# One queue for all transfers of a two-layer decoder step: SyncE issues every DMA, loads are queued when their buffer is free

## The chip, the core and the metric

The kernel runs on one core of a Trainium2 chip. That core has a matrix engine (TensorE, PE in the profile), a vector engine (VectorE, DVE), a scalar engine (ScalarE, ACT), a general one (GpSimd, POOL) and a fifth that only issues transfers and waits (SyncE, SP). Each executes its own list of instructions in order and waits on semaphores for the others. The metric is the device time of one execution in microseconds (us); lower is better.

## The reference

The program is one inference step of a two-layer decoder, for 512 prompt columns and 64 sample columns (8 sequences of 8 tokens) that share all weights. D_MODEL is 1024, and everything is float32. Cut to what matters here:

```
for l in range(2):                              # DEPTH
    h = rmsnorm(x)
    z = h @ w_in[l]                             # all inputs of the mixers, and 4 gates per channel
    A = dilated sliding-window attention, 3 groups of 4 heads; the sample also reads cached keys / values
    B = sliding-window grouped-query attention, 8 heads, window 128; the sample reads its cache
    C = Bc * conv_w3(Cc * hc)                   # the sample starts from state_c_conv
    D = GLU(GELU(Re(C x) + D u)),  x = scan of a complex diagonal state (S5)
    x = x + rmsnorm((sum of gate_i * (branch_i @ W_i)) @ w_out[l])
    x = x + rmsnorm(swiglu(rmsnorm(x)))
    x = x + (p[l] @ w_ple) * sigmoid(x @ w_ple_gate)
return x, and the caches and states moved on by the new positions
```

## The kernel before

**Weights.** All weight products are made with the 576 columns as two halves of 288 (`HS`). A product is three passes of TensorE, high weight times high input, high times low and low times high, so that float32 precision is kept with the fp32r type. Weights arrive as 636 blocks of 128 x 512 (`wblk`, 256 KB each). `load_blk` queues one into a ring of four raw buffers (`wr`, `NRAW`). `split_blk` takes a raw block apart: ACT copies it, rounded, into `wh`, and POOL (or DVE) subtracts to give `wl`; these rings have eight buffers each (`NSPL`). `gemms` emits the products, 24 of 288 columns for a block, 15264 in all, and `pump` queues loads and splits of later blocks whenever a block has had its last product.

**Order.** The program is straight-line code. While it is built, `track` keeps a planned clock for each engine (E, V, S, P, and Q for SyncE) and one for the memory, with a cost for each instruction, and the builder asks these clocks what to emit next: whether VectorE or GpSimd takes an operation (`pick`), and whether a side task may go on (`wait`, `soon`, `calm`). The side tasks are Python generators: the state-space work (`ssm_u`, `ssm_pair`, `ssm_sample`), attention of the prompt (`a_task`, `b_task`), attention of the sample (`sa_task` for mixer A, `sb_task` for B). `tick` advances them between two products of a GEMM, `drain` advances them with no product between when something must be finished first. `PACE` holds numbers that tune this, one set for each layer. What the builder decided is then fixed: each engine executes its list in that order.

**Transfers.** Two engines issue them. `sync` is SyncE: it carries the weight blocks, the stores of new keys and values, states and results, and the copies of the old caches to their outputs (`old_a_k<-cache_a_k` and the like, from DRAM to DRAM). `side_dma` issues all other loads and the scratch traffic from ACT's list: cached keys and values (`kcA`, `vcA`, 52 blocks of 256 KB each in a layer; `kcB`, `vcB`, the mask `mSB`), the three stacked copies of the state-space input that go out to DRAM scratch and come back (`uscr`), their parameters (`bT`, `cT`, `x0`), and the previous convolution inputs (`cpv<-convprev`). `sa_task` keeps up to `PRE` of its blocks queued ahead (6 in the first layer, 7 in the second). A transfer's completion semaphore is one of eight, handed out in the order of the program over both queues, so a transfer waits until the one eight before it has landed.

**Around the change.** The first layer begins with `Gc+A0` and has its state-space work in the background of `A0` and `A1+B`; the second begins with `Gc`. `ep_conv` (mixer C) fetches the convolution state into `cpv`, has POOL copy it to `zcs`, later has POOL gather the new state in `cst` and stores it (`convo`). In the profile all instructions carry line 256, that of the helper that records them, so the names of the tiles tell them apart: `s` are general slots, `bk` PSUM banks, `rc`, `zsw` and `ast` small temporaries.

Of the kernel before, what the change touches and what calls it, by code (L numbers as in the profile page):

```python
# [19 lines left out]
L = 2  # L20
T = 576
# [140 lines left out]
NPAR = 73  # L162
# [105 lines left out]
def _free(ap):  # L268
    n = 1
    for st, c in list(ap.ap)[1:]:  # L270
# [6 lines left out]
    dict(CALM=5.12, ACALM=1.91, RES=6, LOBIAS=11.89, SLACK=-0.07, SIDE_MAX=4, MARGIN=0, PRE=6,  # L277
         CONC=(1, 3, 1, 2, 2), XCALM=0.3, SQP=0.15, NEAR=-0.03, SCALM=4.55, SN=7, HOLD=True, BATCH=1, GR=2),
    dict(CALM=2.03, ACALM=0, RES=1, LOBIAS=8.29, SLACK=0.52, SIDE_MAX=3, MARGIN=3, PRE=7,
         CONC=(3, 4, 2, 2, 1), XCALM=0.3, SQP=-0.3, NEAR=-0.6, SCALM=0, SN=2, HOLD=False, BATCH=1, GR=1),  # L280
# [3 lines left out]
class Build:  # L284
    NS = 63
    NSPL = 8
    SN = 2
# [23 lines left out]
    NEXT = 5  # L311
# [6 lines left out]
    def __init__(self, nc, tc, A, stack):  # L318
# [15 lines left out]
        self.p0 = 0.0  # L334
        self.lat, self.rby = {}, {}
# [45 lines left out]
    def track(self, eng, op, a, k):  # L381
# [20 lines left out]
        if op == "dma_start":  # L402
            self.clk[eng] = t + 0.06
# [4 lines left out]
            e = d + 0.6  # L408
        else:
# [241 lines left out]
    def pump(self):  # L651
        while self.done_blk < self.total_blk and self.uses[self.done_blk] == 0:
            self.wh.pop(self.done_blk)
            self.wl.pop(self.done_blk)
            self.done_blk += 1
        while self.next_split < min(self.total_blk, self.done_blk + self.NSPL):
            if self.next_load <= self.next_split:
                self.load_blk(self.next_load)
                self.next_load += 1
            self.split_blk(self.next_split)  # L660
            self.next_split += 1
        while self.next_load < min(self.total_blk, self.next_split + self.NRAW):
            self.load_blk(self.next_load)
            self.next_load += 1
# [4 lines left out]
    def gemms(self, l, units, half, xs, there=None):  # L669
# [3 lines left out]
        for i in range(n):  # L673
# [4 lines left out]
            for un, bk in zip(units, bks):  # L678
# [9 lines left out]
                if i < n - 1:  # L688
                    if not self.uses[b]:
                        self.pump()  # L690
                    next(self.pre, None)
# [51 lines left out]
    def side_dma(self, o, i):  # L743
        self.S.dma_start(o, i)
# [32 lines left out]
def build(nc, tc, A, stack):  # L777
# [418 lines left out]
    for l in range(L):  # L1196
# [76 lines left out]
        def ep_qkv(un, half, bk):  # L1273
            n, key = un.name, un.key
            c0, w = HS[half]
            if n in ("qa", "ka"):
# [5 lines left out]
                def go():  # L1282
# [3 lines left out]
                    if half == 1:  # L1286
                        while (n, key, 0) not in done:
                            yield None
                        t = (qs if n == "qa" else ks)[:, 2 * key[0] + key[1], :]
# [6 lines left out]
            elif n in ("qb", "kb"):  # L1296
# [10 lines left out]
                def go():  # L1307
# [3 lines left out]
                    if half == 1:  # L1311
                        while (n, key, 0) not in done:
                            yield None
                        if n == "kb":
                            sync.dma_start(A["kvB"][l, 0], s.t)
# [3 lines left out]
            elif n in ("va", "vb"):  # L1319
# [13 lines left out]
                if half == 1:  # L1333
                    o = A["kvA"][l, 1, key[0], key[1]] if n == "va" else A["kvB"][l, 1]
                    sync.dma_start(o, s.t)
                    done.add(("T", n, key))
# [21 lines left out]
        def ep_conv(un, half, bk):  # L1358
# [4 lines left out]
            elif n == "cc":  # L1363
                t = bk.t
                V.tensor_tensor(t[:, :w], bk.t[:, :w], rs1.t[:, c0:c0 + w], OP.mult)
                if i not in zcp:
# [3 lines left out]
                    pv = B.tmp("cpv", 2, (128, 8, 2))  # L1370
                    B.side_dma(pv, A["convprev"][l, :, i])
# [7 lines left out]
                else:  # L1379
# [7 lines left out]
                    cst_ = B.tmp("cst", 2, (128, 18))  # L1387
                    P_.tensor_copy(cst_[:, 0:2], z[:, 512:514])
                    P_.tensor_copy(cst_[:, 2:18].rearrange("p (b k) -> p b k", b=8), zs[:, :, 8:10])
                    sync.dma_start(A["convo"][l, :, i], cst_)  # L1390
# [8 lines left out]
                    B.drop(zcp[i][0])  # L1399
# [39 lines left out]
        def ssm_pair(js):  # L1439
# [6 lines left out]
            for n, j in enumerate(js):  # L1446
                for k in range(3):
                    B.side_dma(braw[n][32 * k:32 * k + 32], A["bT"][l, j])
# [116 lines left out]
        def ssm_sample(jj):  # L1565
# [38 lines left out]
            sync.dma_start(A["ssmS"][l, jj], xs_)  # L1604
# [9 lines left out]
            V.tensor_tensor(xp[:, 1], w1, w2, OP.add)  # L1614
            sync.dma_start(A["ssmP"][l, jj], xp)
            yield from B.wait(X.t, cr.t)
# [853 lines left out]
def make_inputs(inp):  # L2470
# [20 lines left out]
    par[:, :, 72] = np.tile(np.repeat(f["attn_sinks"].reshape(L, 8), 8, axis=1), (1, 2))  # L2491
    m["par"] = par
# [10 lines left out]
    m["bT"], m["cT"] = bT, cT  # L2503
    x0 = np.stack([f["state_d_re"], f["state_d_im"]], 1)
    m["x0"] = np.ascontiguousarray(x0.reshape(L, 2, 8, 2, 4, 128).transpose(0, 3, 5, 1, 4, 2))
    m["convprev"] = np.ascontiguousarray(f["state_c_conv"].reshape(L, 8, 2, 2, 128).transpose(0, 4, 3, 1, 2))
# [71 lines left out]
```

## Time and profile before

| | |
|---|---|
| three runs | 2486.67, 2488.82 and 2489.55 us, median 2488.82 |
| the profiled execution | 2490.76 us; its span, first to last instruction, is 2489.0 |
| PE, DVE, ACT, POOL busy | 2364.5, 1188.9, 985.3, 918.9 us |
| granted TensorE clock, mean over the span | 0.976 of full speed |

Busy time counts neither waits nor the issuing of transfers, which the profile puts on a separate line of the engine's sequencer (ACTq, SPq). A PE that counts as busy can still run at half its clock.

### The profile page before, as it was taken

To read this page: it belongs to the slowest core of one execution; us is meant where nothing else is said; L and a number is where in the kernel's file an instruction comes from. 1 tells how busy PE (TensorE), PEld (TensorE's weight loads), DVE (VectorE), ACT (ScalarE), POOL (GpSimd) and SP (SyncE) were. 2 spreads that over 40 slices of the span, in tenths; PEclk is the share of its full clock that TensorE was granted. 3 is DMA by queue.
4 is the path that set the end of the run, shared out by engine and by line. 5 is a ranking of instruction groups with operands and counts; after the bars stand their busy time and mean duration, and the time that the engine had idled before them with its cause. 6 is when DMAs were issued, how large, how long until landed. Compare 5 with 4: busy or idle time off the path is not lost.

```text
span 2489.0 us, 48194 instructions
## 1 busy us (share of the span) xinstructions
PE 2364.5 (95%) x18686; PEld 2248.7 (90%) x18686; DVE 1188.9 (48%) x3126; ACT 985.3 (40%) x2230; POOL 918.9 (37%) x936
## 2 busy tenths in 40 slices
PE   8899799999999999999997989999999999999999
PEld 8788688877999999999897988998779999999999
DVE  7986897532426220223637798665224342102343
ACT  4333546422346332334532255754223543223342
POOL 5435242222333444433323364422223334344332
PEclk9999899999999999999998999999999999999999
DMA  5334343775453434434444454535874634343332
GB/s 181 100 109 136 105 141 116 247 248 178 136 170 114 119 111 131 125 115 130 142 146 140 127 163 136 154 128 163 278 266 148 203 89 119 115 138 117 115 93 73
DMA packets 164246, 358.94 MB, mean 144 GB/s; under 512 B 25808, under 2 KB 35024, under 8 KB 158800
## 3 DMA queue, kind: packets, MB, share of 16 engines
q1 hardware_dynamic: 118576, 279.08, 36.6%
q10 hardware_dynamic: 45440, 76.77, 9.3%
q8 instruction: 147, 2.41, 0.4%
q14 instruction: 83, 0.68, 0.1%
HBM read 331.59 MB, written 113.43 MB: 179 GB/s over the span
## 4 chain that ended last, share of the span: by engine, by line
PE 73%; DVE 13%; DMA 5%; ACT 3%; issue 3%; POOL 1%; ACTq 1%; SPq 0%; DVEq 0%; POOLq 0%
PE bk L256 73%; DVE s L256 8%; DVE bk L256 4%; DMA s<-vcA 2%; ACT s L256 2%; DMA wr<-wblk 1%; ACTq L256 1%; POOL wl L256 1%; POOL s L256 1%; DMA old_a_k<-cache_a_k 1%; DMA s<-kcA 0%; ACT wh L256 0%; DVE sin L256 0%; DMA cpv<-convprev 0%; DMA s<-uscr 0%
## 5 line engine op out<-in xcount | busy, mean ns | idle before, releaser
L256 PE MATMUL bk<-s,wh 128*128 128x288 f32 x10176 | 2084.0, 300 | 55.0 <-ACT s L256 19.1
L256 PEld LDWEIGHTS bk<-s,wh 128*128 128x128 f32 x10176 | 1647.7, 190 | 95.6 <-issue 29.0
L256 PE MATMUL bk<-s,wl 128*128 128x288 f32 x5088 | 1511.4, 297 | 8.2 <-POOL wl L256 8.2
L256 POOL TENSOR_TENSOR wl<-wr,wh 128x512 fp32r<-128x512 f32 x634 | 817.5, 1297 | 1422.9 <-ACT wh L256 1341.6
L256 PEld LDWEIGHTS bk<-s,wl 128*128 128x128 f32 x5088 | 967.1, 190 | 9.0 <-POOL wl L256 9.0
L256 DVE TENSOR_TENSOR bk<-bk,s 128x288 f32<-128x288 f32 (+2 forms) x620 | 287.5, 481 | 670.3 <-PE bk L256 648.9
L256 ACT ACTIVATE wh<-wr 128x512 fp32r<-128x512 f32 x636 | 396.2, 631 | 392.1 <-PE bk L256 216.2
L256 ACT ACTIVATE s<-bk 128x288 f32<-128x288 f32 (+5 forms) x434 | 171.3, 414 | 414.9 <-DVE bk L256 242.3
L256 PE MATMUL bk<-s,s 128*32 128x128 f32 (+10 forms) x2736 | 192.2, 319 | 32.9 <-DVE s L256 16.8
L256 ACT ACTIVATE zsw<-bk 32x288 f32<-32x288 f32 (+1 forms) x360 | 144.7, 403 | 138.6 <-DVE bk L256 89.7
L256 PEld LDWEIGHTS bk<-s,s 128*32 128x32 f32 (+5 forms) x2736 | 111.3, 130 | 89.5 <-issue 44.1
L256 ACT ACTIVATE rc<-bk 128x288 f32<-128x288 f32 x128 | 52.3, 409 | 278.9 <-DVE bk L256 207.0
L256 DVE TENSOR_TENSOR s<-s,bk 128x288 f32<-128x288 f32 (+1 forms) x226 | 95.1, 440 | 92.3 <-ACT bk L256 89.4
L256 DVE SCALAR_TENSOR_TENSOR s<-bk,s 128x288 fp32r<-128x288 f32 (+1 forms) x184 | 83.0, 456 | 63.1 <-ACT s L256 62.3
L256 PE MATMUL bk<-ident,s 128*128 128x128 f32 (+1 forms) x406 | 65.6, 296 | 20.0 <-ACT s L256 11.5
L256 DVE SCALAR_TENSOR_TENSOR bk<-rc,bk 128x288 f32<-128x288 f32 x96 | 44.2, 460 | 74.1 <-PE bk L256 38.9
L256 PEld LDWEIGHTS bk<-ident,s 128*128 128x128 f32 (+1 forms) x406 | 48.7, 146 | 32.6 <-ACT s L256 14.1
L256 DVE TENSOR_TENSOR s<-bk,s 128x512 f32<-128x512 f32 (+3 forms) x124 | 66.1, 572 | 24.9 <-PE bk L256 24.6
L256 DVE TENSOR_TENSOR s<-s,s 128x32 f32<-128x32 f32 (+8 forms) x221 | 73.7, 375 | 6.5 <-DMA s<-cT 4.4
L256 DVE COPY s<-bk 128x512 f32<-128x512 f32 (+5 forms) x102 | 47.2, 471 | 61.8 <-PE bk L256 40.5
L256 ACT ACTIVATE s<-bk,par 128x288 fp32r<-128x288 f32 (+1 forms) x80 | 41.4, 517 | 63.5 <-PE bk L256 35.0
L256 ACT ACTIVATE s<-s,bst 128x256 f32<-128x256 f32 (+1 forms) x87 | 40.1, 473 | 43.6 <-DVE bst L256 43.6
(114 smaller groups left out, 976.0 us busy)
## 6 DMA issues: line engine op xcount, KB each, us to landing
wr<-wblk SPq DMA_DIRECT2D x636, 256.0 KB
old_a_k<-cache_a_k SPq DMA_DIRECT2D x128, 255.0 KB
old_a_v<-cache_a_v SPq DMA_DIRECT2D x128, 255.0 KB
s<-kcA ACTq DMA_DIRECT2D x104, 256.0 KB
s<-vcA ACTq DMA_DIRECT2D x104, 256.0 KB
old_a_k<-cache_a_k SPq DMA_DIRECT2D x32, 252.0 KB
old_a_v<-cache_a_v SPq DMA_DIRECT2D x32, 252.0 KB
kvA<-s SPq DMA_DIRECT2D x24, 288.0 KB
```

Source lines behind the costliest of these rows:

```text
L256: r = f(*a, **k)
```

## The change

1. `side_dma` issues from SyncE. ACT issues no transfer any more (376 before).
2. A new `fetch`, called from `pump` and between the products of a GEMM, queues a weight block only when the planner thinks that the last reader of its raw buffer is nearly done; before, `pump` queued it as soon as the ring's numbering allowed.
3. The planner gives a transfer 0.4 us of issue instead of 0.06, and holds the ninth open transfer of SyncE's queue until the first has landed (`lanes`). `NEXT` and the numbers in `PACE` are other ones; `sa_task` queues 8 blocks ahead in the second layer (7 before).
4. GpSimd's copies of new queries, keys and convolution state, and the stores of `kvA`, `kvB`, `convo`, `ssmS` and `ssmP`, are emitted when the planner thinks that their data is there (`B.wait`), as side tasks where they weren't.
5. The convolution state comes as 32 more columns of the parameter tile `par`, so the four `convprev` loads are gone.
6. `bT` is stacked three times on the host: one load of 96 x 256 in place of three of 32 x 256 (48 become 16).

The number of weight products and their order are unchanged, and so is the other arithmetic.

```diff
@@ -274,10 +274,10 @@
 PACE = (
...
-    dict(CALM=2.03, ACALM=0, RES=1, LOBIAS=8.29, SLACK=0.52, SIDE_MAX=3, MARGIN=3, PRE=7,
-         CONC=(3, 4, 2, 2, 1), XCALM=0.3, SQP=-0.3, NEAR=-0.6, SCALM=0, SN=2, HOLD=False, BATCH=1, GR=1),
+    dict(CALM=1.41, ACALM=0.0, RES=1, LOBIAS=14, SLACK=0.21, SIDE_MAX=3, MARGIN=3, PRE=8,
+         CONC=(2, 4, 2, 2, 2), XCALM=0.3, SQP=0.23, NEAR=-0.6, SCALM=0, SN=5, HOLD=True, BATCH=1, GR=1),
@@ -400,12 +401,17 @@
             t = max(t, self.fin.get(y, self.base.get(y[0], 0.0)) + (0.0 if f[1] == eng else f[0]),
                     self.rdt.get(y, 0.0) + (0.0 if self.rby.get(y, eng) == eng else 0.13))
         if op == "dma_start":
-            self.clk[eng] = t + 0.06
+            if eng == "Q":
+                self.lanes.append(0.0)
+                t = max(t, self.lanes.popleft())
+            self.clk[eng] = t + 0.4
             by = n * list(outs[0].ap)[0][1] * 4 / 340e3
             lat = 0.1
             self.clk["D"] = max(self.clk["D"], self.now) + by
             d = max(self.clk["D"], t + 1.4 + by)
             e = d + 0.6
+            if eng == "Q":
+                self.lanes[-1] = e
         else:
             lat = 0.13
             if eng == "E":
@@ -659,7 +665,13 @@
                 self.next_load += 1
             self.split_blk(self.next_split)
             self.next_split += 1
+        self.fetch()
+
+    def fetch(self):
         while self.next_load < min(self.total_blk, self.next_split + self.NRAW):
+            old = self.ring.get(("wr", self.ring.get(("n", "wr"), 0) % self.NRAW))
+            if self.last.get(old, 0.0) > self.now + 0.2:
+                break
             self.load_blk(self.next_load)
             self.next_load += 1
 
@@ -688,6 +700,7 @@
                 if i < n - 1:
                     if not self.uses[b]:
                         self.pump()
+                    self.fetch()
                     next(self.pre, None)
                     self.nt += 1
                     self.tick(self.nt % self.BATCH == 0)
@@ -741,7 +754,7 @@
             self.RES if any(st["q"] for st in self.streams[1:]) else 0), "room")
 
     def side_dma(self, o, i):
-        self.S.dma_start(o, i)
+        self.Q.dma_start(o, i)
 
     def booked(self):
         return sum(max(0, a[1]) for st in self.streams for a in st["act"])
@@ -1286,6 +1299,7 @@
                     if half == 1:
                         while (n, key, 0) not in done:
                             yield None
+                        yield from B.wait(s.t)
                         t = (qs if n == "qa" else ks)[:, 2 * key[0] + key[1], :]
                         P_.tensor_copy(t, s.t[:, 512:576])
                         if n == "ka":
@@ -1312,6 +1326,7 @@
                         while (n, key, 0) not in done:
                             yield None
                         if n == "kb":
+                            yield from B.wait(s.t)
                             sync.dma_start(A["kvB"][l, 0], s.t)
                         done.add((n, key))
 
@@ -1332,8 +1347,13 @@
                     ep_scale(bk, s.t[:, c0:c0 + w], half)
                 if half == 1:
                     o = A["kvA"][l, 1, key[0], key[1]] if n == "va" else A["kvB"][l, 1]
-                    sync.dma_start(o, s.t)
-                    done.add(("T", n, key))
+
+                    def go():
+                        yield from B.wait(s.t)
+                        sync.dma_start(o, s.t)
+                        done.add(("T", n, key))
+
+                    B.task(go())
 
         def v_task(n, key):
             s = vT.pop((n, key))
@@ -1367,8 +1387,7 @@
                     B.room(1)
                     zcp[i] = (B.slot(), cp.tile([128, 80], F32, name=B.nm("zcs"), tag=f"zcs{i}"))
                     V.memset(zcp[i][0].t[:, 0:2], 0.0)
-                    pv = B.tmp("cpv", 2, (128, 8, 2))
-                    B.side_dma(pv, A["convprev"][l, :, i])
+                    pv = pr[:, 73 + 16 * i:89 + 16 * i].rearrange("p (b k) -> p b k", b=8)
                     zs = zcp[i][1].rearrange("p (b k) -> p b k", b=8)
                     P_.tensor_copy(zs[:, :, 0:2], pv)
                 z = zcp[i][0].t
@@ -1384,10 +1403,6 @@
                     B.pdrop(bk)
                     B.drop(hcs[i])
                     y = dst(yc, i)
-                    cst_ = B.tmp("cst", 2, (128, 18))
-                    P_.tensor_copy(cst_[:, 0:2], z[:, 512:514])
-                    P_.tensor_copy(cst_[:, 2:18].rearrange("p (b k) -> p b k", b=8), zs[:, :, 8:10])
-                    sync.dma_start(A["convo"][l, :, i], cst_)
                     yp = y.t[:, 0:512]
                     yS = y.t[:, 512:576].rearrange("p (b k) -> p b k", b=8)
                     cw = [convw[:, 2 * k + i:2 * k + i + 1] for k in range(3)]
@@ -1396,7 +1411,17 @@
                     for k in (1, 2):
                         V.scalar_tensor_tensor(yp, z[:, k:k + 512], cw[k], yp, op0=OP.mult, op1=OP.add)
                         V.scalar_tensor_tensor(yS, zs[:, :, k:k + 8], cw[k], yS, op0=OP.mult, op1=OP.add)
-                    B.drop(zcp[i][0])
+
+                    def go():
+                        yield from B.wait(z, zcp[i][1])
+                        cst_ = B.tmp("cst", 2, (128, 18))
+                        P_.tensor_copy(cst_[:, 0:2], z[:, 512:514])
+                        P_.tensor_copy(cst_[:, 2:18].rearrange("p (b k) -> p b k", b=8), zs[:, :, 8:10])
+                        B.drop(zcp[i][0])
+                        yield from B.wait(cst_)
+                        sync.dma_start(A["convo"][l, :, i], cst_)
+
+                    B.task(go())
             else:
                 t = bk.t[:, :w]
                 V.tensor_tensor(t, t, rs1.t[:, c0:c0 + w], OP.mult)
@@ -1444,8 +1469,8 @@
             urs = [B.slot() for _ in js]
             braw = [br.t[0:96] for br in brs]
             for n, j in enumerate(js):
+                B.side_dma(braw[n], A["bT"][l, j])
                 for k in range(3):
-                    B.side_dma(braw[n][32 * k:32 * k + 32], A["bT"][l, j])
                     B.side_dma(urs[n].t[32 * k:32 * k + 32], uscr[l][jj, k, 32 * (j % 4):32 * (j % 4) + 32])
             bts, us = [], []
             for n in R2:
@@ -1601,7 +1626,6 @@
             xs_ = sc.t[:, 0]
             for i in range(2):
                 W.tensor_copy(xs_[:, i], pv[i])
-            sync.dma_start(A["ssmS"][l, jj], xs_)
             xp = B.tmp("xpo", 2, (128, 2, 4))
             w1, w2 = (keep.t[:, spare + o_:spare + o_ + 4] for o_ in (16 * jj, 16 * jj + 8))
             f = ssm.xf[:, :, js]
@@ -1612,8 +1636,9 @@
             V.tensor_tensor(w1, f[:, 0], ki, OP.mult)
             V.tensor_tensor(w2, f[:, 1], kr, OP.mult)
             V.tensor_tensor(xp[:, 1], w1, w2, OP.add)
+            yield from B.wait(X.t, cr.t, sc.t, xp)
+            sync.dma_start(A["ssmS"][l, jj], xs_)
             sync.dma_start(A["ssmP"][l, jj], xp)
-            yield from B.wait(X.t, cr.t)
             (b1,) = yield from B.banks(1, True)
             for k in range(4):
                 o = b1.t[32 * k:32 * k + 32, 0:64]
@@ -2489,6 +2514,7 @@
     par[:, :, 62:64] = cols(f["ssm_d"], 2)
     par[:, :, 64:72] = f["attn_sinks"].reshape(L, 1, 8)
     par[:, :, 72] = np.tile(np.repeat(f["attn_sinks"].reshape(L, 8), 8, axis=1), (1, 2))
+    par[:, :, 73:105] = f["state_c_conv"].reshape(L, 8, 2, 2, 128).transpose(0, 4, 3, 1, 2).reshape(L, 128, 32)
     m["par"] = par
     bT = np.zeros((L, 8, 32, 2, 128), np.float32)
     cT = np.zeros((L, 128, 2, 8, 32), np.float32)
@@ -2500,10 +2526,9 @@
                 r0 = 16 * gg
                 bT[:, j, r0:r0 + 16, i, 64 * gg:64 * gg + 64] = b[:, g].transpose(0, 2, 1)
                 cT[:, 64 * gg:64 * gg + 64, i, j, 16 * gg:16 * gg + 16] = c[:, g].transpose(0, 2, 1)
-    m["bT"], m["cT"] = bT, cT
+    m["bT"], m["cT"] = np.ascontiguousarray(np.tile(bT, (1, 1, 3, 1, 1))), cT
     x0 = np.stack([f["state_d_re"], f["state_d_im"]], 1)
     m["x0"] = np.ascontiguousarray(x0.reshape(L, 2, 8, 2, 4, 128).transpose(0, 3, 5, 1, 4, 2))
-    m["convprev"] = np.ascontiguousarray(f["state_c_conv"].reshape(L, 8, 2, 2, 128).transpose(0, 4, 3, 1, 2))
     kc = np.zeros((L, 2, 13, 2, 128, 4, 128), np.float32)
     vc = np.zeros((L, 2, 13, 2, 128, 2, 256), np.float32)
     c0 = 0
```

Places where the rows of an engine's list move, as the two kernels order them. The number behind a name counts the tiles, so the same work has another number in the changed kernel.

ACT before, at the opening of the second layer; behind these nine rows follow 22 more transfers of `bT` and `uscr`, and then the four `uscr` writes of the second half, before the next weight copy `wh_15270`:

```order
L256 ACTIVATE wh_15174<-wr_15103 128x512
L256 ACTIVATE s_15185<-s_15054 128x576
L256 ACTIVATE s_15192<-s_15056 128x576
L256 DMA uscr_115<-s_15185 128x576
L256 DMA uscr_115<-s_15186 128x576
L256 DMA uscr_115<-s_15185 128x576
L256 DMA uscr_115<-s_15054 128x576
L256 DMA s_15212<-bT 32x256
L256 DMA s_15214<-uscr_115 32x576
```

ACT of the changed kernel at the same place:

```order
L256 ACTIVATE wh_15152<-wr_15102 128x512
L256 ACTIVATE s_15156<-s_15039 128x576
L256 ACTIVATE s_15167<-s_15041 128x576
L256 ACTIVATE wh_15242<-wr_15120 128x512
L256 ACTIVATE wh_15259<-wr_15138 128x512
L256 ACTIVATE s_15323<-s_15194 96x576
```

The weight copies now follow at once. SP of the changed kernel there; behind these ten rows come the same eight for the second half, two cache copies and the next weight load:

```order
L256 DMA wr_15165<-wblk 128x512
L256 DMA wr_15183<-wblk 128x512
L256 DMA uscr_115<-s_15156 128x576
L256 DMA uscr_115<-s_15157 128x576
L256 DMA uscr_115<-s_15156 128x576
L256 DMA uscr_115<-s_15039 128x576
L256 DMA s_15192<-bT 96x256
L256 DMA s_15194<-uscr_115 32x576 x3
L256 DMA s_15193<-bT 96x256
L256 DMA s_15195<-uscr_115 32x576 x3
```

What stood between ACT's copies is now a run of 26 transfers on SP without a weight load.

ACT before, in the sample's attention of the first layer (`bst`, `sast`: softmax statistics of B and of the sample's A):

```order
L256 ACTIVATE bst_5997<-bst_5997 128x4
L256 DMA s_6026<-vcA 128x512
L256 DMA s_6028<-vcA 128x512
L256 DMA s_6030<-vcA 128x512
L256 DMA s_6032<-vcA 128x512
L256 ACTIVATE s_5542,sast_5433<-s_5542,sast_5433 128x320
```

SP of the changed kernel in that stretch:

```order
L256 DMA wr_6521<-wblk 128x512
L256 DMA old_a_k<-cache_a_k 16x4080
L256 DMA s_6537<-kcB 128x512
L256 DMA s_6539<-vcB 128x512
L256 DMA s_6538<-kcB 128x512
L256 DMA s_6540<-vcB 128x512
L256 DMA s_6545<-mSB 128x768
L256 DMA s_6565<-kcA 128x512
L256 DMA s_6567<-kcA 128x512
L256 DMA s_6594<-kcA 128x512
```

The cached keys and values now stand in one list with the weight blocks and the cache copies.

PE of the changed kernel at the drain ahead of `Gb` in the first layer, where 2544 accumulation steps of the GEMMs (of three products each) are done; before, these rows of `sb_task` lay partly among GEMM rows:

```order
L256 MATMUL bk_6507<-s_4816,wl_5902 128x288
L256 MATMUL bk_6523<-s_6492,s_3012 64x128 x4
L256 MATMUL bk_6523<-s_6493,s_3012 64x128 x4
L256 MATMUL bk_6476<-s_6464,s_6447 32x128 x4
L256 MATMUL bk_6476<-s_6466,s_6447 32x128 x4
L256 MATMUL bk_6476<-ks_247,s_6447 128x64 x3
L256 MATMUL bk_6476<-ks_247,s_6448 128x64 x3
L256 MATMUL bk_6577<-s_6468,s_6447 32x128 x4
L256 MATMUL bk_6577<-s_6470,s_6448 32x128 x4
```

PE before at a drain of the second layer (10176 steps done), where the whole of `sb_task` stands without a product between; in the changed kernel it is spread over the steps from 9993 to 10035:

```order
L256 MATMUL bk_20699<-s_19409,wl_20220 128x288
L256 MATMUL bk_20717<-s_20598,s_20608 64x128 x2
L256 MATMUL bk_20717<-s_17937,s_20608 128x64
```

So the drain of the second layer moves out and one comes into the first.

## Rows read from the trace of the kernel before

**Rows 1.** The page: busy time of the engines, and the last chain by engine.

```profile
PE 2364.5 (95%) x18686; PEld 2248.7 (90%) x18686; DVE 1188.9 (48%) x3126; ACT 985.3 (40%) x2230; POOL 918.9 (37%) x936
...
PE 73%; DVE 13%; DMA 5%; ACT 3%; issue 3%; POOL 1%; ACTq 1%; SPq 0%; DVEq 0%; POOLq 0%
```

**Rows 2.** The core's span and mean granted TensorE clock.

```profile
core 0: 2489.0 us, clock 0.976
```

**Rows 3.** Tiles: transfer issues, shortest, median and longest in ns.

```profile
L256 ACTq DMA_DIRECT2D s<-vcA x104: 334/442/1640, 468.0 to 1851.5; - x104
...
L256 SPq DMA_DIRECT2D wr<-wblk x636: 327/328/1112, 1.6 to 2455.7; - x159
```

**Rows 4.** ACT's timeline, second layer's opening: start, duration, [idle before, releaser].

```profile
1283.83 2.80 ACTq L256 DMA_DIRECT2D uscr<-s  x4
...
1306.77 0.63 ACT L256 ACTIVATE wh<-wr 128x512 fp32r<-128x512 f32 x1 [22.39 <-DMA uscr<-s]
```

**Rows 5.** SP's timeline there.

```profile
1285.01 21.11 SPq L256 DMA_DIRECT2D old_a_k<-cache_a_k  x2
```

**Rows 6.** POOL's timeline there.

```profile
1316.08 0.20 POOL L256 COPY zcs<-cpv 128x16 f32<-128x16 f32 x1 [7.34 <-DMA cpv<-convprev]
1325.57 0.20 POOL L256 COPY zcs<-cpv 128x16 f32<-128x16 f32 x1 [9.29 <-DMA cpv<-convprev]
```

**Rows 7.** PE's timeline there, the two long gaps.

```profile
1327.03 0.61 PE L256 MATMUL bk<-s,wl 128*128 128x288 f32 x1 [6.90 <-POOL wl L256]
...
1338.56 1.10 PE L256 MATMUL bk<-s,wh 128*128 128x288 f32 x2 [5.88 <-ACT s L256]
```

**Rows 8.** Busy time by stretch: a full one, then that opening.

```profile
core 0: us, PE busy (x) PEld busy (x) DVE busy (x) ACT busy (x) POOL busy (x), PEclk, DMA share, GB/s
950.00:1000.00 50.00, 50.00 (x379) 50.00 (x379) 1.40 (x3) 13.55 (x27) 20.50 (x16) 1.00 0.48 148
...
1305.00:1345.00 40.00, 23.95 (x128) 22.85 (x129) 22.05 (x57) 12.28 (x24) 13.07 (x15) 0.74 0.47 149
```

**Rows 9.** The same view: attention and state-space work of the first layer.

```profile
230.00:292.00 62.00, 45.85 (x387) 38.47 (x389) 50.28 (x153) 25.32 (x55) 16.05 (x27) 0.78 0.34 103
```

**Rows 10.** PE's timeline there, the gaps over 3 us after 250 us.

```profile
254.94 1.11 PE L256 MATMUL bk<-ident,s 128*128 128x128 f32 x4 [3.15 <-DVE s L256]
...
259.49 1.12 PE L256 MATMUL bk<-ident,s 128*128 128x128 f32 x4 [3.44 <-ACT s L256]
...
279.39 1.11 PE L256 MATMUL bk<-ident,s 128*128 128x128 f32 x4 [3.67 <-ACT s L256]
...
285.72 1.11 PE L256 MATMUL bk<-ident,s 128*128 128x128 f32 x4 [3.03 <-ACT s L256]
```

**Rows 11.** ACT's timeline there, its longest hold.

```profile
247.16 1.67 ACT L256 ACTIVATE wh<-wr 128x512 fp32r<-128x512 f32 x3 [7.70 <-DMA s<-uscr]
```

**Rows 12.** Busy time by stretch: the sample's attention, first and second layer.

```profile
436.00:596.00 160.00, 149.25 (x1473) 121.75 (x1472) 59.90 (x189) 53.47 (x147) 36.44 (x48) 0.96 0.75 246
...
1715.00:1732.00 17.00, 15.15 (x107) 11.18 (x107) 7.31 (x26) 5.43 (x19) 6.63 (x17) 0.80 0.52 158
1732.00:1862.00 130.00, 125.83 (x1247) 97.87 (x1247) 31.86 (x77) 31.20 (x69) 31.06 (x36) 1.00 0.83 283
...
1800.00:1850.00 50.00, 46.74 (x485) 36.07 (x488) 10.85 (x28) 10.93 (x25) 10.27 (x9) 1.00 0.91 313
```

**Rows 13.** Waits in the whole span: us in total, times, longest.

```profile
PE bk L256 <- ACT s L256: 32.3, 11, 5.9
...
ACT wh L256 <- DMA s<-bT: 18.6, 2, 15.7
...
PE bk L256 <- DMA s<-vcA: 8.4, 10, 1.6
```

**Rows 14.** Busy time around ACT's second-longest hold, 15.7 us.

```profile
1410.00:1427.00 17.00, 17.00 (x130) 17.00 (x129) 6.42 (x11) 1.28 (x3) 7.50 (x20) 1.00 0.64 176
```

**Rows 15.** SP's own waits in the whole span: us in total, times, longest.

```profile
SPq L256 <- POOL wl L256: 1473.7, 571, 22.0
```

More of the change, by code (lines that the diff above doesn't have):

```diff
@@ L161 @@
 COPY_FROM, COPY_TO = 24, int(0.95 * N_STEPS)
-NPAR = 73
+NPAR = 105
 B_GAP = 0.005
@@ L276 @@
 PACE = (
-    dict(CALM=5.12, ACALM=1.91, RES=6, LOBIAS=11.89, SLACK=-0.07, SIDE_MAX=4, MARGIN=0, PRE=6,
-         CONC=(1, 3, 1, 2, 2), XCALM=0.3, SQP=0.15, NEAR=-0.03, SCALM=4.55, SN=7, HOLD=True, BATCH=1, GR=2),
-    dict(CALM=2.03, ACALM=0, RES=1, LOBIAS=8.29, SLACK=0.52, SIDE_MAX=3, MARGIN=3, PRE=7,
-         CONC=(3, 4, 2, 2, 1), XCALM=0.3, SQP=-0.3, NEAR=-0.6, SCALM=0, SN=2, HOLD=False, BATCH=1, GR=1),
+    dict(CALM=5.12, ACALM=1.89, RES=4, LOBIAS=7.86, SLACK=-0.07, SIDE_MAX=4, MARGIN=0, PRE=6,
+         CONC=(1, 3, 1, 2, 2), XCALM=0.3, SQP=-0.3, NEAR=-0.03, SCALM=4.55, SN=3, HOLD=False, BATCH=3, GR=2),
+    dict(CALM=1.41, ACALM=0.0, RES=1, LOBIAS=14, SLACK=0.21, SIDE_MAX=3, MARGIN=3, PRE=8,
+         CONC=(2, 4, 2, 2, 2), XCALM=0.3, SQP=0.23, NEAR=-0.6, SCALM=0, SN=5, HOLD=True, BATCH=1, GR=1),
 )
@@ L310 @@
     SQP = 0.0
-    NEXT = 5
+    NEXT = 6
     NEAR = 0.0
@@ L334, in __init__ @@
         self.p0 = 0.0
+        self.lanes = deque([0.0] * 8)
         self.lat, self.rby = {}, {}
```

## Prediction

> **What bounds the kernel.** I read the page's busy times first. TensorE is busy for 2364.5 of 2489.0 us, and the last chain is 73% TensorE [rows 1]. So a gain can only come out of two things: the 124.5 us in which it stands (2489.0 - 2364.5), and the time that it loses at a low clock. Its granted clock has two levels, full (2.4 GHz) and half (1.2 GHz); the mean is 0.976 [rows 2], and a microsecond at half speed does half a microsecond of work, so (1 - 0.976) x 2489 = 60 us are lost that way. Together 184 us are the ceiling.
>
> Next I asked what ScalarE's list does while it issues. An issue takes 442 ns at the median [rows 3]; 376 of them are an estimated 166 us in which ScalarE splits no weights, although its busy time, 985.3 us, looks idle enough. Whether that costs anything depends on where the holds fall, which only the timeline tells. I read it where TensorE stands.
>
> **A, opening of the second layer.** ScalarE issues the first `uscr` write at 1283.83 and splits the next weight block at 1306.77, 22.39 us idle by the profile [rows 4]. Meanwhile SyncE stands for 21.11 us at two cache copies [rows 5]: the completion semaphores go round over both queues, so its transfers wait for ScalarE's. TensorE lives on split blocks through most of this, then starves: GpSimd stands 7.34 and 9.29 us for the convolution state [rows 6] with weight subtractions behind it, and TensorE stands 6.90 us for a low weight and 5.88 us for an evacuation [rows 7]. The full stretch does 379 TensorE instructions in 50 us; the 40 us from 1305 hold 128, at clock 0.74 [rows 8], which would be 128/379 x 50 = 16.9 us of work at full speed. 23.1 us are lost.
>
> The change takes every part of this chain away: 32 issues leave ScalarE there (8 writes, 24 reads), the convolution state needs no transfer, and GpSimd's copies are emitted later. What replaces it is the run of 26 issues on SyncE; at 0.44 us that is 11.4 us, plus two round trips through scratch, with no weight load between. Its cover: a block holds 24 products, 24/379 x 50 = 3.2 us of TensorE, and up to four raw and eight split blocks lie ahead, 38 us when the rings are full. If they were empty, the whole 11.4 us would show. I take **-20**, bounds -23 and -9 (20 less 11.4).
>
> **B, state-space work beside attention in the first layer.** In the 62 us from 230, TensorE stands 16.2 us and the clock is 0.78, which loses up to 0.22 x 62 = 13.6 us: together 30 [rows 9]. The four gaps sum to 13.3 us [rows 10]. ScalarE's hold of 7.70 us [rows 11] comes just ahead of the first two; those, 6.6 us, and a quarter of the clock's loss, 3.4 us, I credit to it. The last two gaps come when ScalarE has long been free, and VectorE is busy for 50.28 of the 62 us; they stay. **-10**, bounds 0 (VectorE sets all four) and -20 (two thirds of 30).
>
> **C, the sample's attention in the first layer.** From 436 to 596 TensorE stands 10.8 us and loses 0.04 x 160 = 6.4 us to the clock: 17 [rows 12]. ScalarE issues 104 blocks here, standing when the semaphore round makes it wait. I credit 13 of the 17. Against it stands the new drain ahead of `Gb`, where `sb_task` runs with no products between. The nearest row is the second layer's drain: in 17 us there TensorE stands 1.9 us and loses 0.2 x 17 = 3.4 us, 5.3 in all [rows 12]. So **-8**; bounds -17 and +5.
>
> **D, the sample's attention in the second layer.** That drain is spread out: -5. The 130 us behind it move 283 GB/s; the densest 50 us reach 313 [rows 12], so the same bytes need 283/313 x 130 = 117.5 us, and no more than 12.5 us can be had, of which TensorE's standing (4.2 us) is what I count. **-9**; bounds 0 and -17.
>
> **E, the rest.** TensorE waits 32.3 us for ScalarE's `s` in all [rows 13]; 16.0 of that were counted (5.88, 3.44, 3.67, 3.03). A third of the remaining 16.3 comes from ScalarE being behind: **-5**, bounds 0 and -16. Not everything that holds ScalarE counts: its second-longest hold, 15.7 us for `bT` [rows 13], falls where TensorE is busy for 17.00 of 17 us at clock 1.00 [rows 14]. The larger `par` tile, the merged `bT` loads (32 fewer issues) and the stores put behind a wait cost nothing: they lie on SyncE and GpSimd, and a store delays only what is queued behind it, a weight load, covered as in A while the rings are full. The planner's numbers have no row of their own; they enter by the drains, in C and D.
>
> **Given back.** In the two attention stretches SyncE now issues 104 x 0.442 us of cached blocks, some 22 weight loads at 0.33 and 10 cache copies at 0.5 us (weights and copies an estimate from the order): 58 us of 130. It is not full, but a blocked weight load now stands ahead of keys and values. TensorE's waits on `vcA` are 8.4 us in all now [rows 13]; I take them to double, and keys to add a little: **+10**, bounds 0 and +50 (rival 2).
>
> The Trainium skill, page "DMA: Bandwidth & Descriptors", section "Issuing engines are not separate DMA queues", says that issuing on several engines saves only the sequencer's time, which is usually small beside the transfer. By it the sum would be nil (rival 3); the trace differs at A, where one run of issues keeps ScalarE from its other work for 22.39 us.
>
> **Sum.** -20 - 10 - 8 - 9 - 5 + 10 = -42 us. The profiled execution took 2490.76 us, 1.94 above the median 2488.82, so it gives 2448.8 on its own scale and **2447** on the median's.
>
> **Rivals.**
>
> 1. *Partial gain, 2471.* VectorE or the rings take over where ScalarE's holds end. For it: VectorE is busy for 50.28 of 62 us in B and 22.05 of 40 in A. Against it: TensorE's gaps in A are ended by weights. Half of A (-10), a third of B (-3) and -5 for all else: -18.
> 2. *Slower, 2497.* One in-order queue: a weight load that is queued before its raw buffer is free holds up the cached blocks. SyncE stands 1473.7 us in 571 such waits, 2.6 each, up to 22.0 [rows 15]; today they hold no cached block, since those go through ScalarE. In the second layer 104 blocks go in 130 us, 1.25 each, and eight ahead cover 10 us; in the first, 160/104 = 1.54 and six cover 9.2. A hold of 22 then costs 12 to 12.8. From three holds on (-42 + 37) the gain is gone; two in each layer give +8. Against it: `fetch` queues a load only when the planner thinks the buffer is free, and the mean wait is far under the cover. The page's section "Queues, rings and completion order" of the Trainium skill adds that each DMA engine takes turns between queue rows, so cached blocks also lose their separate turn; no run here shows that yet.
> 3. *No change, 2489.* The issues were hidden, and what TensorE waited for moves elsewhere. For it: rows 14, where a 15.7 us hold cost nothing. Against it: the chain in A, which is shown link by link.
> 4. *Larger, 2414.* Nothing is given back and most of the lost time comes home: A -23, B -18, C -12, D -12, E -10 = -75. For it: the shorter waits keep the clock up, since in A and B the clock fell behind the gaps. Against it: each term is then near its bound.
>
> **Chances.** Forecast (2435 to 2460) 0.40; partial (2460 to 2484) 0.25; larger (below 2435) 0.17; no change 0.06; slower 0.12. With 0.2% (5 us) as what a measurement can tell here, faster is 0.82, same 0.06, slower 0.12. The range leaves out the slower cases and the far end of the larger: 2402 to 2486. The likeliest case's own range is 2435 to 2460.
>
> **What the profile would show.** A: no idle of ScalarE over 8 us at the second layer's opening, weight splits going on there, over 250 TensorE instructions in the 40 us (303 would be the full rate). B: the two gaps behind ScalarE's hold gone, the other two there. C: the drain ahead of `Gb` as a stretch at a clock below 0.9. D: none at its old place, and over 283 GB/s behind it. Given back: TensorE's waits on `vcA` and `kcA` between 8 and 20 us. I am wrong if SyncE's run of 26 issues empties the weight rings, if TensorE's waits for cached blocks exceed 40 us, or if the gaps in A return with VectorE as releaser.

## Result and profile after

The changed kernel takes 2432.66 us (median of 4 runs, 2430.76 to 2435.29), the kernel before 2489.19 beside it: a ratio of 0.9775, 95% interval 0.9759 to 0.9792, which is 56.5 us less. The forecast was 2447, range 2402 to 2486. So it lies inside the range, just below the likeliest case's own (2435 to 2460), in what the prediction called its larger case (0.17). That the total came near is luck in part: beside its own term, the second layer's opening came out 21 us worse, the state-space work of the first layer 6 us worse, the two attention stretches 15 us better and all other places 25 us better.

The profiled execution has a span of 2433.5 us, 55.5 below that of before. First the page, as in [rows 1], with the line of the queues:

```profile
PE 2343.5 (96%) x18686; PEld 2239.5 (92%) x18686; DVE 1169.4 (48%) x3100; ACT 992.8 (41%) x2245; POOL 929.6 (38%) x947
...
q1 hardware_dynamic: 162928, 355.85, 45.9%
...
PE 80%; DVE 11%; DMA 2%; ACT 2%; issue 2%; POOL 1%; SPq 1%; DVEq 0%; ACTq 0%; POOLq 0%
```

SyncE's queue carries everything now, and the share of transfers in the last chain fell from 5% to 2%. TensorE stands for 90.0 us (2433.5 - 2343.5) in place of 124.5, and its mean clock is 0.981 in place of 0.976.

Because TensorE does the same 15264 weight products in the same order, the two traces can be laid beside each other by that count. I read the time at which the n-th product starts in each; the last column is what a stretch gained.

| products | stretch that ends there | before | changed | difference | in the stretch |
|---|---|---|---|---|---|
| 1000 | first layer's opening | 179.1 | 172.7 | -6.4 | -6.4 |
| 2250 | attention and state space, first layer | 439.0 | 420.3 | -18.7 | -12.3 |
| 3000 | sample's attention, first layer | 622.8 | 594.4 | -28.4 | -9.7 |
| 7750 | the rest of the layer | 1279.0 | 1249.7 | -29.4 | -1.0 |
| 8250 | second layer's opening | 1371.2 | 1343.1 | -28.1 | +1.3 |
| 9750 | state space, second layer | 1628.6 | 1588.6 | -40.0 | -11.9 |
| 11000 | sample's attention, second layer | 1898.3 | 1845.8 | -52.5 | -12.5 |
| end | the rest | 2489.0 | 2433.5 | -55.5 | -3.0 |

The opening of the second layer, where the forecast put its largest gain, gained nothing. Its timelines in the changed kernel, of SP, ACT and PE (start, duration, [idle before, releaser]):

```profile
1255.70 2.12 SPq L256 DMA_DIRECT2D uscr<-s  x4
...
1273.91 1.33 SPq L256 DMA_DIRECT2D old_a_k<-cache_a_k  x2
1275.34 1.21 SPq L256 DMA_DIRECT2D wr<-wblk  x2
...
1278.01 0.82 SPq L256 DMA_DIRECT2D wr<-wblk  x2
...
1288.51 3.47 SPq L256 DMA_DIRECT2D wr<-wblk  x2
```

```profile
1269.12 0.63 ACT L256 ACTIVATE wh<-wr 128x512 fp32r<-128x512 f32 x1 [0.97 <-PE bk L256]
1286.49 0.63 ACT L256 ACTIVATE wh<-wr 128x512 fp32r<-128x512 f32 x1 [16.73 <-DMA wr<-wblk]
...
1296.86 0.63 ACT L256 ACTIVATE wh<-wr 128x512 fp32r<-128x512 f32 x1 [7.17 <-DMA wr<-wblk]
1297.40 0.39 ACT L256 ACTIVATE s<-bk 128x288 fp32r<-128x288 f32 x1
...
1307.84 0.63 ACT L256 ACTIVATE wh<-wr 128x512 fp32r<-128x512 f32 x1 [8.65 <-DMA wr<-wblk]
```

```profile
1297.84 1.10 PE L256 MATMUL bk<-s,wh 128*128 128x288 f32 x2 [7.03 <-ACT s L256]
1309.98 0.85 PE L256 MATMUL bk<-s,wh 128*128 128x288 f32 x2 [6.70 <-ACT s L256]
```

SyncE's run without a weight load lasts from 1255.70 to 1275.34, 19.6 us; the prediction's 11.4 were the issues alone, without the two round trips through scratch. Worse, the load issued at 1275.34 reaches ScalarE at 1286.49: it took 11.0 us to land, against a median of 2.8. The tile's row (from issue to landing, of the 76 loads out of 636 whose landing the trace tells):

```profile
DMA to landing us min/median/max: 2.5/2.8/11.0
```

So ScalarE is no longer held by its own issues, as in [rows 4], but for 16.73 us by a late block. TensorE still works through this hold, until 1290.8. Its two gaps, of about the size of those in [rows 7], stand behind the next loads. The blocks issued at 1278.01 and 1288.51 are split at 1296.86 and 1307.84 (loads and splits are in the same order, so the n-th load belongs to the n-th split): ScalarE's waits for them end 18.7 and 19.2 us after the issue. The evacuation `s<-bk` that ends TensorE's first gap stands right behind the first of these splits in ScalarE's list.

What makes the blocks late stands next to them in the queue: the small cache copies, which the trace's list of packets shows as four pieces of 61,440 bytes each, 2.27 us long at the median and, at this opening, never more than two at once. The seven small copies around it are 28 such pieces, 66.9 us of transfer, of which the last ends at 1306. That a weight block queued among them has to wait for those two is a reading, which a_copy below tests. The kernel before issues the same copies at the same place.

Busy time by stretch, beside [rows 8, 9 and 12]: the opening, state space beside attention, the first layer's drain, the second layer's sample attention.

```profile
1278.00:1312.00 34.00, 19.55 (x123) 18.21 (x122) 18.00 (x58) 9.66 (x21) 8.47 (x10) 0.84 0.36 122
210.00:257.00 47.00, 43.30 (x388) 39.93 (x388) 34.08 (x93) 28.08 (x60) 23.67 (x45) 0.96 0.50 151
...
495.00:519.00 24.00, 19.56 (x237) 14.05 (x235) 6.77 (x27) 3.86 (x14) 8.10 (x26) 0.79 0.84 298
1677.00:1810.00 133.00, 132.19 (x1343) 107.69 (x1342) 36.60 (x88) 35.65 (x78) 41.22 (x54) 1.00 0.84 298
```

And the waits for cached keys and values in the whole span, TensorE's, then SyncE's (us, times, longest):

```profile
PE bk L256 <- DMA s<-kcA: 0.8, 1, 0.8
```

```profile
SPq L256 <- DMA s<-kcA: 14.1, 45, 0.9
```

No row of TensorE's matmuls waiting for `vcA` is left; it was 8.4 us in [rows 13].

### The profile page after: what moved, and what is told of

The parts are those of the page before. It is cut to its first block, busy times and chain, and to the rows that moved or that the text cites. A ratio compares the mean times of both kernels' runs of the same rounds, so it can differ in the third digit from the quotient of the medians.

```text
span 2433.5 us, 48402 instructions
## 1 busy us (share of the span) xinstructions
PE 2343.5 (96%) x18686; PEld 2239.5 (92%) x18686; DVE 1169.4 (48%) x3100; ACT 992.8 (41%) x2245; POOL 929.6 (38%) x947
## 4 chain that ended last, share of the span: by engine, by line
PE 80%; DVE 11%; DMA 2%; ACT 2%; issue 2%; POOL 1%; SPq 1%; DVEq 0%; ACTq 0%; POOLq 0%
PE bk L256 80%; DVE s L256 8%; DVE bk L256 3%; DMA wr<-wblk 2%; ACT s L256 1%; SPq L256 1%; ACT wh L256 0%; DMA s<-cT 0%; POOL wl L256 0%; POOL s L256 0%; ACT zsw L256 0%; DVE bst L256 0%; DMA s<-kcA 0%; ACT bk L256 0%; ACT L256 0%
## 5 line engine op out<-in xcount | busy, mean ns | idle before, releaser
L256 ACT ACTIVATE s<-bk 128x288 fp32r<-128x288 f32 (+5 forms) x456 | 181.4, 416 | 406.0 <-DVE bk L256 237.7
L256 PE MATMUL bk<-s,s 128*64 128x128 f32 (+8 forms) x2736 | 184.8, 319 | 20.1 <-DVE s L256 14.8
L256 PEld LDWEIGHTS bk<-s,s 128*32 128x32 f32 (+4 forms) x2736 | 110.6, 130 | 71.9 <-issue 44.3
L256 DVE TENSOR_TENSOR s<-bk,s 128x512 f32<-128x512 f32 (+3 forms) x124 | 66.1, 572 | 23.9 <-PE bk L256 23.7
L256 DVE TENSOR_TENSOR s<-s,s 128x32 f32<-128x32 f32 (+8 forms) x221 | 68.6, 351 | 4.0 <-ACT s L256 1.2
L256 DVE COPY s<-bk 128x512 f32<-128x512 f32 (+6 forms) x80 | 35.8, 451 | 55.8 <-PE bk L256 38.7
```

Of the source, the lines that this page charges most:

```text
L256: r = f(*a, **k)
```

## Experiments

Three things had to be told apart: whether the engine that issues matters (theory 1, the prediction's), or the order of the work (theory 2), and what bounds the second opening (theory 3, the cache copies). Ratios are against the kernel before, run beside each, with 95% intervals.

| run | edit | us | ratio |
|---|---|---|---|
| changed | | 2432.7 | 0.9775 [0.9759, 0.9792] |
| b_sp | before, all transfers on SyncE | 2482.6 | 0.9977 [0.9962, 0.9993] |
| b_late | b_sp, weight loads queued late | 2480.9 | 0.9975 [0.9962, 0.9988] |
| a_act | changed, side transfers on ScalarE | 2482.4 | 0.9979 [0.9961, 0.9997] |
| a_early | changed, weight loads queued early | 2482.2 | 0.9983 [0.9972, 0.9994] |
| a_pace | changed, old `PACE` and `NEXT` | 2446.8 | 0.9847 [0.9832, 0.9862] |
| a_no4 | changed without part 4 | 2449.9 | 0.9843 [0.9826, 0.9860] |
| b_small | before with parts 5 and 6 | 2471.2 | 0.9939 [0.9923, 0.9956] |
| b_copy | before, small copies spread | 2469.8 | 0.9921 [0.9904, 0.9938] |
| a_copy | changed, small copies spread | 2420.5 | 0.9723 [0.9705, 0.9740] |
| a_copy_ssm | a_copy, `uscr` and `bT` on ScalarE | 2430.1 | 0.9767 [0.9751, 0.9784] |
| b_latecopy | b_late, small copies spread | 2453.0 | 0.9855 [0.9834, 0.9877] |
| a_copyord | a_copy, largest cache copied first | 2421.0 | 0.9727 [0.9710, 0.9745] |

In b_sp, b_late, b_copy, b_latecopy, a_act, a_early, a_copy, a_copy_ssm and a_copyord the work of TensorE, VectorE and GpSimd stands in the order of the kernel that they come from, and ScalarE's but for the transfers; only the issuing of transfers differs. The others are planned anew, so the whole order shifts with them.

### The queue alone

An issuer is given whose instructions the planner books as it did:

```diff
+        self.QS = Eng(self, nc.sync, "S")
...
-        self.S.dma_start(o, i)
+        self.QS.dma_start(o, i)
```

> The kernel before with every transfer that ScalarE issued issued by SyncE, all other work in its old order. If ScalarE's holds are the cost (theory 1), most of the gain comes with this alone: 2440 to 2465 us. If the order and the later queueing of weight loads are what gains (theory 2), it is within 10 us of 2489. If weight loads queued before their buffer is free hold up the cached keys and values (rival 2 of the prediction), it is slower than before: 2495 to 2560, with TensorE waiting for vcA and kcA for over 40 us.

4 us came, not 24 to 49: theory 1 fails in this form. Nor is it slower, so the slower rival falls too, though it has part of a point: TensorE's waits for `kcA` grew from 2.3 to 7.8 us.

```profile
PE bk L256 <- DMA s<-kcA: 7.8, 13, 1.9
```

The same edit backwards, in the changed order:

```diff
+        self.SQ = Eng(self, nc.scalar, "Q")
...
-        self.Q.dma_start(o, i)
+        self.SQ.dma_start(o, i)
```

> The changed kernel with the same transfers given back to ScalarE, all other work in the changed order. Theory 1: 35 to 50 us of the gain are lost, 2468 to 2483 us. Theory 2: the engine that issues matters little, 2428 to 2443.

Nearly the whole gain goes, 2482.4, as theory 1 had it here, so theory 2 fails as well: the order alone is worth 4 us. By product count, a_act loses 23.0 us against the changed kernel between the 2250th and the 3000th product, 19.2 between the 9750th and the 11000th, and -1.0 at the second opening (7750 to 8250). It is the sample's attention that pays. ScalarE's waits for cached blocks in a_act:

```profile
ACT s L256 <- DMA s<-vcA: 27.5, 5, 8.6
ACT wh L256 <- DMA s<-kcA: 24.9, 5, 9.1
ACT rc L256 <- DMA s<-vcA: 24.7, 4, 8.9
ACT rc L256 <- DMA s<-kcA: 20.4, 4, 7.2
```

97.5 us in 18 waits; in the changed kernel 7.5 us of such waits are left on ScalarE. The kernel before has 85.3 us of them, and b_sp none, so their going is not enough by itself. SyncE suffers with it, because the round of completion semaphores spans both queues: its waits for `kcA`, here of a_act, have a longest of 23.7 us, against 0.9 above.

```profile
SPq L256 <- DMA s<-kcA: 58.0, 13, 23.7
```

### The late queueing of weight loads

In b_late each weight load keeps its place in the plan, but is emitted only when `fetch`'s condition holds. In a_early each is emitted as soon as the numbering allows; its place in the plan stays.

```diff
+            if b > need and self.last.get(old, 0.0) > self.now + 0.2:
+                break
+            self.late.popleft()
+            self.Q.eng.dma_start(t, src)
```

> The kernel before with all transfers on SyncE, as in the run b_sp (2482.6 us), and each weight load moved down SyncE's list to where the planner thinks that its buffer is free; all other lists as before. Theory 1b: one queue pays only when no weight load stands in it unready, so the sample's attention gains here what b_sp did not: 2440 to 2470 us. Rival: the changed order of the work is what lets it gain: within 6 us of b_sp, 2477 to 2489.

```diff
+        while len(self.early) < min(self.total_blk, self.next_split + self.NRAW):
+            self.real_load()
```

> The changed kernel with the weight loads moved up SyncE's list to where the ring's numbering allows them, as before the change; all other lists as they are. Theory 1b: they stand unready ahead of the cached keys and values, 15 to 42 us are lost: 2448 to 2475. Rival: 2428 to 2440.

a_early loses 49.5 us, more than its expectation allowed, and again in the sample's attention (21.6 us between the 2250th and the 3000th product). SP's timeline there in a_early:

```profile
506.99 1.01 SPq L256 DMA_DIRECT2D s<-vcA  x2
518.62 0.33 SPq L625 DMA_DIRECT2D wr<-wblk  x1
519.05 2.75 SPq L256 DMA_DIRECT2D s<-kcA  x6
```

A weight load stands there from 508.00 to 518.62 for its buffer, and six key blocks right behind it. This is the slower rival's mechanism, at work: TensorE's waits for `kcA` and `vcA` are 10.5 and 8.4 us in a_early. `fetch` is what keeps it out of the changed kernel.

b_late did not gain what was expected; its number is the rival's, but its places are not. It gains 19.9 us on b_sp between the 2250th and the 3000th product, where TensorE's granted clock is 1.00 (0.97 in b_sp), and loses 12.9 between the 8000th and the 8250th, and 9.4 between the 750th and the 1000th. Its blocks come late at the openings (ScalarE's waits, b_late):

```profile
ACT wh L256 <- DMA wr<-wblk: 115.9, 24, 33.4
```

The longest, 33.4 us, is not all landing. SyncE stands from 1295.0 to 1311.88 at a store of `convo`, whose data stand behind GpSimd's waits of 28.85 and 4.42 us for the convolution state; only then is the block queued, at 1313.00, and it lands within 7.2 us. So without part 4 a store that is not ready holds SyncE's list just as a weight load does.

### The cache copies

```diff
-COPY_PIECES = {"a1": (2, 1), "a2": (1, 2), "a3": (1, 8), "b": (4, 1)}
+COPY_PIECES = {"a1": (8, 4), "a2": (1, 2), "a3": (1, 8), "b": (8, 2)}
```

The same number of copies with the same bytes, each 8 pieces of 30,720 bytes in place of 4 of 61,440.

> The changed kernel with the copies of the two smallest caches cut into 8 packets of 30 KB in place of 4 of 61 KB, same bytes and same order. Theory 3: at the second layer's opening these copies keep two DMA engines busy for some 30 us, and weight loads land behind them; spread out, 10 to 25 us come back there: 2408 to 2423. If the opening is bounded by something else: 2433 within 5.

> The kernel before with the same cut of the copies. Theory 3: the opening of its second layer gains as well, 5 to 25 us: 2464 to 2484. If ScalarE's hold of 22 us alone bounds that opening, as the prediction has it: 2489 within 5.

Both gain where theory 3 puts it: 12.1 us on the changed kernel, 11.5 of them between the 7750th and the 8250th product, and 16.6 on the kernel before, 12.7 of its profiled execution's at that place. In a_copy eight pieces run at a time, the last ends at 1283 rather than 1306, the longest landing of a weight block is 5.1 us where the trace tells it (the tile's row, a_copy), and the two loads that took 18.7 and 19.2 us take 6.5 and 6.7:

```profile
DMA to landing us min/median/max: 2.5/2.7/5.1
```

In the kernel before, the first of TensorE's two gaps stood behind the convolution state [rows 6, 7]. That was late for the same reason: in b_copy GpSimd's waits for it at this place, 7.34 and 9.29 us, shrink to this (timeline, b_copy).

```profile
1298.62 0.37 POOL L256 COPY zcs<-cpv 128x16 f32<-128x16 f32 x2 [0.58 <-DMA cpv<-convprev]
```

What is left in a_copy I put down to VectorE, busy for 23.46 of 24 us there (by stretch); no run tests that:

```profile
1276.00:1300.00 24.00, 19.11 (x125) 18.88 (x124) 23.46 (x63) 10.40 (x21) 9.11 (x11) 0.86 0.54 174
```

With the copies out of the way, the prediction's term A can be tried by itself:

```diff
-                B.side_dma(uscr[l][jj, k], z.t.bitcast(F32))
+                B.SQ.dma_start(uscr[l][jj, k], z.t.bitcast(F32))
...
-                B.side_dma(braw[n], A["bT"][l, j])
+                B.SQ.dma_start(braw[n], A["bT"][l, j])
```

> The run a_copy (2420.5 us: the changed kernel with the small cache copies spread) with the state-space transfers alone, uscr and bT, issued by ScalarE again; all lists otherwise the same. Term A of the prediction: ScalarE's hold at the second layer's opening costs some 20 us, and with the copies out of the way it must show: 2432 to 2442 us. Theory 3: that opening was bounded by the copies and then by VectorE, the hold costs little: 2416 to 2427.

9.6 us, between the two expectations. ScalarE is held for 19.17 us again (its timeline, a_copy_ssm), and the opening (7750 to 8250) loses 7.5 us by it, a later state-space stretch (8500 to 8750) 3.2.

```profile
1270.10 1.15 ACT L256 ACTIVATE wh<-wr 128x512 fp32r<-128x512 f32 x2 [19.17 <-DMA old_a_k<-cache_a_k]
```

So a hold of 19 us costs TensorE some 7, since split blocks cover most of it. The copies are also what stood in b_late's way:

> The run b_late (2480.9 us) with the small cache copies spread over 8 packets. It gained 26 us in the sample's attention and lost 19 at the second layer's opening, where weight loads land up to 33 us late. Theory 3: they sit behind the copies; spread, 15 to 25 us come back: 2456 to 2466. If its late loads are late by the planner's clock: 2475 to 2483.

27.9 us come back, somewhat more than the 15 to 25 expected, 21.1 of them between the 8000th and the 8250th product, and ScalarE's waits for weight blocks fall from 115.9 to 51.2 us. The whole is now 34 us below the kernel before, with that kernel's order. Against b_copy (2469.8), which has the copies spread too, one queue with late loads is worth 17 us there.

Moving the spread copies out of the openings as well brings nothing more:

```diff
-        for n in ("a1", "a2", "a3", "b"):
+        for n in ("a3", "a2", "b", "a1"):
```

> The run a_copy with the list of cache copies in another order, the largest cache first and the small ones of mixer A last in each layer, so that they leave both openings. Theory 3: what is left of the copies at the opening goes, 0 to 6 us: 2414 to 2421 us. Rival: the copies that come in their place cost as much: 2419 to 2424.

2421.0 beside a_copy's 2420.5: no difference that can be told; it fits the rival, and theory 3's range at its upper end.

### The rest of the change

> The changed kernel with the old numbers in PACE and NEXT, planned anew. Theory 1b: the numbers are worth little, 2425 to 2448 us. Rival: the numbers carry the gain, 2460 to 2489.

> The kernel before with parts 5 and 6 alone (convolution state in the parameter tile, one bT load in place of three), planned anew. The prediction puts them at nothing by themselves, but the waits for the convolution state at the second layer's opening go, 16.6 us on GpSimd: 2479 to 2489 us. Rival: they carry that opening's gain, under 2475.

> The changed kernel without part 4 (stores and GpSimd's small copies emitted as soon as their code is reached), planned anew. The prediction puts part 4 at nothing: 2428 to 2440 us. Rival: in one queue an unready store holds up the cached keys and values: 2443 to 2470.

The old numbers in `PACE` cost 14 us, at the upper end of what was expected if they matter little. Without part 4 it is 17 us slower, in the rival's range, where the prediction had nothing. The rival's path is not seen, though: TensorE's waits for `kcA` are 1.8 us, and the first layer's attention (2250 to 3000) is 5.8 us faster. The loss lies before the 2250th product (16.3 us) and between the 8250th and the 9750th (5.2). In the whole span SyncE waits 160.6 us for VectorE's `s`, which the stores carry out, against 95.3, and ScalarE 65.5 us for weight blocks against 49.9 (SyncE's row, a_no4, below). This fits unready stores that delay weight loads, but since the plan is new as well, it is not shown.

```profile
SPq L256 <- DVE s L256: 160.6, 42, 12.5
```

Parts 5 and 6 gain 15 us on the kernel before, again in the rival's range, but only 5.7 of its profiled execution's between the 7750th and the 8500th product. Each of the three shifts the whole plan, so a size here is that of the edit with its new order.

## Why the prediction came out near, point by point

**A (-20)** is the step that failed. It held that ScalarE's issues and the convolution transfers bound the second layer's opening, and that "every part of this chain" goes. They went, and TensorE's gaps stayed: the opening lost 1.3 us. Transfers that land late beside the cache copies bound it in both kernels: the convolution state and then a weight block before, weight blocks after. I had the copies in [rows 5] as a victim of ScalarE's issues and did not ask how long they take to land. The cover that I counted, 38 us of blocks ahead, lasted through SyncE's run of 19.6 us and the 11.0 of landing behind it, but not through the next two landings of 18.7 and 19.2 us. The prediction's own sign of being wrong, that the run of 26 issues empties the weight rings, came true: ScalarE has no block to split from 1269.75 to 1286.38. With the copies spread, the hold is worth 7 to 10 us (a_copy_ssm), a third to half of the term.

**Given back (+10)** had the wrong sign. TensorE's waits for keys and values did not double, from 10.7 us (8.4 and 2.3) they fell to 0.8. I had one queue down as a cost for them; a_act and a_early show that it pays, if no unready weight load stands in it: ScalarE's 97.5 us of waits for cached blocks, and SyncE's waits across queues, go with it.

**C and D (-8 and -9)** were right in place, and with what is given back they make -7 for the two stretches; measured are -9.7 and -12.5, together -22.2. The mechanism was half of it: b_sp takes ScalarE's issues away and gains nothing in these stretches against the kernel before (+0.8 and +3.3 us), and only with late weight loads, in b_late, 19.1 and 3.4 us come. The drain ahead of `Gb` is there, at clock 0.79, and dearer than its price of 5.3 us: 4.4 us of standing and 5.0 of clock. The second layer's stretch moves 298 GB/s at clock 1.00, up from 283.

**B (-10)**: all the gaps of [rows 10] are gone, those that I gave to VectorE too, and the clock is 0.96 in place of 0.78; but part of it was only moved. Between the 1250th and the 1750th product 4.3 us are left. **E (-5)** was far too small: outside the places named, 30.3 us came: 9.9 before the 1250th product, 4.5 from 1750 to 2250, 1.0 from 3000 to 7750, 11.9 from 8250 to 9750 and 3.0 at the end. Most of it does not come from the engine that issues: a_act, with ScalarE issuing again, still gains 24.0 of these 30.3 us on the kernel before, while it loses 20.0 in the two attention stretches. So parts 2 to 6 and the new order gain elsewhere about what they cost in the attention while ScalarE issues, and the one queue takes that cost away. Which of these parts brings how much stays open; a_no4 and b_small, planned anew, say only that parts 4 to 6 are not without effect.

The slower rival was real: a_early, which differs in the place of the weight loads alone, loses 49.5 us. The rival of no change is what each half by itself gives: b_sp and a_act are both within 0.3% of before.

The Trainium skill, page "DMA: Bandwidth & Descriptors", section "Issuing engines are not separate DMA queues", which says that several issuing engines save only sequencer time, fits b_sp, where the move is worth 0.2%. It does not cover a_act, where the same transfers on ScalarE cost 2% with everything else in the same order.

## What to carry to other kernels

An issue queue is an in-order list: put transfers into one only if each is queued when it can start, and then the waits across queues go away; here the queue alone was worth 0.2%, the rest of the change without it 0.2%, and both 2.2%. Stores need the same care (b_late). When a load lands late, look at what shares its queue and how many pieces of that run at once, before blaming the engine that issues. Two traces of the same work are best compared at equal counts of that work: the total of this forecast hid errors of 15 to 25 us, which cancelled in part.

## What was unexpected of the hardware

The small DRAM-to-DRAM copies all move 245,760 bytes in 4 pieces of 61,440, but not alike. Those of mixer A's smallest cache (`a1`), two rows of 122,880 bytes each by the kernel's code, run two pieces at a time at the opening; those of mixer B's (`b`), four rows of 61,440, run four at a time (1213 to 1232 us in the changed kernel). Cut into eight rows of 30,720, eight run at a time. So here the number at once went with the rows of the copy, not with the number of its pieces.

256 KB loads queued among the copies that run two at a time reach ScalarE 11.0, 18.7 and 19.2 us after their issue, where the median landing is 2.8. Spreading the copies makes the changed kernel 12 us faster: a_copy, 2420.5 us, ratio 0.9723 [0.9705, 0.9740], is faster than both kernels.
